# Keeping the residual in the output rows and adding the last sums there by accumulating transfers

## The chip, the core and the metric

The kernel runs on one of the eight cores of a Trainium2 chip. A core has engines that run their own instruction lists side by side and wait for each other through semaphores: TensorE (PE in the profile, its weight loads PEld) multiplies matrices into PSUM, VectorE (DVE), ScalarE (ACT) and GpSimd (POOL) work element by element, and SyncE (SP) here only issues transfers. The metric is the device time of one launch in microseconds (us). Several runs were timed; one more execution was recorded by the profiler.

## The reference

One layer of a hybrid backbone on 128 context tokens and 512 latent tokens, 1,024 channels each. A mixer sub-layer (pooling and neighbourhood attention, merged by gates) gives a first residual, then a channel sub-layer adds to it. Cut to what matters here:

```python
x = x + ga * _merge(pool, na, gp, gn, w_pool_proj, w_na_proj, w_o)
h = _modulated_norm(x, norm_ffn_g, sf, cf)
x = x + gf * _conv_ffn(h, w_up, ffn_conv_w, ffn_conv_b, w_down)
```

`_conv_ffn` is an up-projection to 2 x 2,816 channels, a width-3 convolution over positions, `silu(a) * g`, and a down-projection. The change is about the last line: the `x` on its right is the residual, and its left side is the output, `y_prompt` for the context tokens (rows `yc`) and `y_sample` for the latent ones (rows `yl`).

## The kernel before

All matrices are float32. Each product is made of three matmuls on operands that are split into a high part and a remainder (`split_to`, L132: ACT casts the high part, L133, DVE subtracts it, L134). The 640 tokens are five tiles of 128: tile 0 the context, tiles 1 to 4 the latent tokens.

The end of the program is the channel sub-layer. `out_product` (L731) makes `x1`, the residual, tile by tile, and L742 stores each tile to a scratch tensor `xscr` in DRAM, since the buffers of `x1` are given up afterwards. The up-projection then runs in 22 blocks of 128 + 128 channels (`up_a`, `up_w`, `products_b`, `up_b`). Each block multiplies in a scheme with fewer products: POOL forms four combinations `ws` of its weights (L858 to L861, `up_a`), `up_w` splits them, `products_b` multiplies and combines the results into `ua` and `ug` (`ug` at L887 by DVE, with a copy `p5` of a partial product by ACT, L885). `up_b` then convolves (`conv`: ACT at L925, DVE taps at L926 and L927), applies silu (ACT, L942), multiplies (L943, POOL, for the last block DVE) and splits into `ahi` and `alo` (in the last block `th` and `tl`, in the place of older tiles).

Two blocks make a group for the down-projection: `down_weights` loads and splits its two weight tiles, `down_group` multiplies and adds into an SBUF tile `acc` of five token tiles by 1,024. There are 11 groups. Up to group 8 (`GATED`) the sums are added without the gate `gf`. Then `join` (L952) runs over all ten pieces of `acc` (five tiles, two halves of 512 columns): POOL multiplies the piece with the gate (L953), SP loads the piece of the residual back from `xscr` into one of three small buffers `xr` (L955), and POOL adds it (L956). Group 9, and tile 0 of group 10, multiply the new sum with the gate on DVE (L998) and add it on POOL (L999). The other tiles of group 10 use weights that were multiplied with the gate beforehand (POOL, L973), so DVE only adds (L1001). SP stores each finished piece to the output (L1006); tile 4 goes in pieces of 256 columns.

Weights come through `load_raw` (L124) into three buffers `raw` of 512 KB; the gated weight tiles take buffers of the same three. A load waits until the buffer's last reader is done, and all plain transfers stand in one list on SP, in order. The order of each engine's instructions is set ahead of the run by a scheduler that works from a model of the machine, so a change in one place can reorder the instructions around it on several engines. The program was recorded with `schedule_with_timeline_sim=True`.

Of the kernel before, what the change touches and what calls it, by code (L numbers as in the profile page):

```python
# [10 lines left out]
F32 = mybir.dt.float32  # L11
# [6 lines left out]
P = 128  # L18
D = 1024
# [40 lines left out]
def tok_cols(t):  # L60
    return slice(t * P, (t + 1) * P)
# [3 lines left out]
def body(ctx, tc, A):  # L65
    nc = tc.nc
    MULT, ADD, SUB, MIN = ALU.mult, ALU.add, ALU.subtract, ALU.min
# [6 lines left out]
    def pool(stack, name, bufs=1, side="left", space=bass.MemoryType.SB):  # L74
        return stack.enter_context(tc.tile_pool(name=name, bufs=bufs, space=space, reuse_waits="tile",
                                                side=side if space == bass.MemoryType.SB else None))
# [16 lines left out]
    mraw = const.tile([P, 4, 2, 8], F32, name="mraw")  # L93
    dscr = pool(ctx, "dscr", space=bass.MemoryType.DRAM)
    gscr = dscr.tile([2, 16, P], F32, name="gscr")
    xscr = dscr.tile([P, 5, D], F32, name="xscr")
    qg8 = const.tile([P, 1], F32, name="qg8")
    nc.vector.tensor_scalar(out=bca1[:, 0:8], in0=vec[:, V_BCA:V_BCA + 8], scalar1=1.0, scalar2=None, op0=ADD)
    nc.vector.tensor_scalar(out=qg8, in0=vec[:, V_QG:V_QG + 1], scalar1=DH ** -0.5, scalar2=None, op0=MULT)
# [13 lines left out]
    def ps_acc():  # L113
        return PS.tile([P, 512], F32, tag="acc", name="acc", bufs=NACC)
# [224 lines left out]
    for t in range(5):  # L339
        dst = VX if t == 0 else V[t - 1]  # L340
# [293 lines left out]
    for g in range(4):  # L634
        d = pool_group(g)
# [55 lines left out]
    x1 = fp.tile([P, 5, D], F32, name="x1")  # L691
# [17 lines left out]
    def residual(ps, t, chunk, sq):  # L709
        sl = slice(chunk * 512, (chunk + 1) * 512)  # L710
        tmp = fp.tile([P, 512], F32, name="o_t", bufs=2)
        nc.vector.tensor_tensor(out=tmp, in0=ps, in1=gab[:, 1 if t == 0 else 0, sl], op=MULT)
        if chunk == 0:
            nc.gpsimd.tensor_tensor(out=x1[:, t, sl], in0=x1[:, t, sl], in1=tmp, op=ADD)
        else:
            nc.vector.tensor_tensor(out=x1[:, t, sl], in0=x1[:, t, sl], in1=tmp, op=ADD)
        nc.scalar.activation(tmp, x1[:, t, sl], AF.Square, accum_out=sq[:, t:t + 1])
# [6 lines left out]
    for u in range(4):  # L724
        r = load_raw(A["wo"][4 + u])
        sl = slice(2 * u, 2 * u + 2)
        split_to(two(r), w1h[:, sl, :], w1l[:, sl, :])
    for t in range(5):
        residual(acc[t], t, 0, sq0)

    def out_product(t, mid):  # L731
        ps = ps_acc()
        for kt in range(KT):
            if kt == MID and t:
                mid(t - 1)
            xh, xl = mhi[:, kt, tok_cols(t)], mlo[:, kt, tok_cols(t)]
            nc.tensor.matmul(ps, lhsT=xh, rhs=w1h[:, kt, :], start=(kt == 0), stop=False)
            nc.tensor.matmul(ps, lhsT=xh, rhs=w1l[:, kt, :], start=False, stop=False)
            nc.tensor.matmul(ps, lhsT=xl, rhs=w1h[:, kt, :], start=False, stop=(kt == KT - 1))
        residual(ps, t, 1, sq1)  # L740

        nc.sync.dma_start(xscr[:, t, :], x1[:, t, :])  # L742
        std = fp.tile([P, 1], F32, name="std2", bufs=2)
        nc.vector.tensor_tensor(out=std, in0=sq0[:, t:t + 1], in1=sq1[:, t:t + 1], op=ADD)
        nc.scalar.activation(std, std, AF.Sqrt, bias=eps, scale=1.0 / D)
        nc.vector.reciprocal(std, std)
        xn = fp.tile([P, D], F32, name="xn2", bufs=2)
        nc.scalar.activation(xn, x1[:, t, :], AF.Copy, scale=std)
        return xn
# [56 lines left out]
    for t in range(5):  # L806
        xns.append(out_product(t, lambda t: second_h(t, xns[t])))
        if t >= 3:
            sums(*J[t - 3])
# [141 lines left out]

    def join(o, gate, t, sl):  # L952
        nc.gpsimd.tensor_tensor(out=o, in0=o, in1=gate, op=MULT)  # L953
        xr = fr.tile([P, 512], F32, tag="xr", name="xr", bufs=3)
        nc.sync.dma_start(xr, xscr[:, t, sl])  # L955
        nc.gpsimd.tensor_tensor(out=o, in0=o, in1=xr, op=ADD)  # L956

    def down_weights(g):
# [20 lines left out]
    def down_group(g, xs, ws, gated):  # L979
        last = g == NG - 1  # L980
        for t in range(5):
            c0 = 0 if t == 0 else C_LAT - 1 + (t - 1) * P
            n = CUT if last and t == 4 else 512
            for c in range(0, D, n):
                sl = slice(c, c + n)
                ps = (ps_acc if g >= NG - 2 and (c // 512 + t) % 2 else ps_small)()[:, :n]
                for j, (hi, lo) in enumerate(gated if last and t else ws):
                    xh, xl = [x[:, c0:c0 + P] for x in xs[j]]
                    nc.tensor.matmul(ps, lhsT=xh, rhs=hi[:, sl], start=(j == 0), stop=False)  # L989
                    nc.tensor.matmul(ps, lhsT=xh, rhs=lo[:, sl], start=False, stop=False)  # L990
                    nc.tensor.matmul(ps, lhsT=xl, rhs=hi[:, sl], start=False, stop=(j == GRP - 1))  # L991
                o = acc[:, t, sl]
                gate = gfb[:, 1 if t == 0 else 0, sl]
                if g == 0:
                    nc.vector.tensor_copy(o, ps)
                elif g > GATED and (t == 0 or not last):
                    tmp = fr.tile([P, 512], F32, tag="xr", name="xr", bufs=3)
                    nc.vector.tensor_tensor(out=tmp, in0=ps, in1=gate, op=MULT)  # L998
                    nc.gpsimd.tensor_tensor(out=o, in0=o, in1=tmp, op=ADD)  # L999
                else:  # L1000
                    nc.vector.tensor_tensor(out=o, in0=ps, in1=o, op=ADD)  # L1001
                if g == GATED:
                    gating.append((o, gate, t, sl))
                if last:
                    dst = A["yc"] if t == 0 else A["yl"][(t - 1) * P:t * P, :]
                    nc.sync.dma_start(dst[:, sl], o)  # L1006

    pend = []
    for f in range(NF):
        if 1 < f + 1 < NF:  # L1010
            up_a(f + 1)
        nxt = up_b(f)
        if 1 < f + 1 < NF:
            up_w(f + 1)
        if f == NF - 2:
            for a in gating[5:]:
                join(*a)
        elif f == NF - 3:
            for a in gating[:5]:
                join(*a)  # L1020
        g = f // GRP - 1
        if f >= NF - 2:
            pend.append(nxt)
            continue
        if f % GRP == 0 and g >= 0:
            down_group(g, pend, *down_weights(g))
            pend = []
        pend.append(nxt)
    w2, w1 = down_weights(NG - 2), down_weights(NG - 1)
    with tc.issue_after(upped[0]):  # L1030
        down_group(NG - 2, pend[:GRP], *w2)
    down_group(NG - 1, pend[GRP:], *w1)
    e6.close()

# [96 lines left out]
```

## Time and profile before

| | us |
|---|---|
| median of 3 runs | 928.6 (926.58 to 931.41) |
| the profiled execution | 925.25 |
| its span, first to last instruction | 923.5 |
| PE busy in the span | 873.9 (95%) |
| DVE busy | 680.4 (74%) |
| ACT busy | 397.0 (43%) |
| POOL busy | 280.3 (30%) |

The span is what the trace covers; the profiled execution's own time is 1.75 us longer. A matmul counts as busy until its modelled end, so a busy PE says that PE wasn't waiting, not that it ran at its peak. The shares are averages over very different stretches; over the last tenth of the span they say little. In the rows, L and a number is a line of the kernel, `x10` a count, and `[4.28 <-ACT whi L133]` says that the engine had been idle for 4.28 us and which instruction's end released it.

### The profile page before, as it was taken

Reading aid. Unit: us, or ns where it says so; the run is one execution under the profiler, and the core shown is the slowest. Engines: PE = TensorE matmul, PEld = TensorE weight load, DVE = VectorE, ACT = ScalarE, POOL = GpSimd, SP = SyncE. Lnnn points to the kernel's source line nnn. Section 1 sums busy time; section 2 is a strip of 40 time slices with the busy share of each in tenths; the row PEclk is TensorE's granted clock in tenths of the full one; section 3 lists DMA queues with packets and bytes.
Section 4 is the critical chain, followed back from the end, with each engine's and each line's share of the span. In section 5 each row is a group of like instructions: output and inputs, shape, how many; then the busy total and the mean of one; then the engine's idle time right before and its main releaser. Section 6 shows DMA issues by size and latency. Waiting matters only on the chain.

```text
span 923.5 us, 13399 instructions
## 1 busy us (share of the span) xinstructions
PE 873.9 (95%) x5234; PEld 783.5 (85%) x5234; DVE 680.4 (74%) x998; ACT 397.0 (43%) x712; POOL 280.3 (30%) x206
## 2 busy tenths in 40 slices
PE   3799999999998999999889899999999999999688
PEld 2578898887898999988689799999999999898677
DVE  3456986897479633535699888879788797887696
ACT  4351344445443422225766453635435354453340
POOL 2122000000000021322206434444334543339956
PEclk9999999999999999999989999999999999999989
DMA  8758425664365222264222421213222141222213
GB/s 235 248 206 270 153 75 171 200 227 137 104 197 159 73 84 73 70 233 155 92 69 103 137 78 59 92 61 122 70 69 92 46 136 51 89 92 80 92 45 115
DMA packets 33024, 112.20 MB, mean 121 GB/s; under 512 B 3857, under 2 KB 4529, under 8 KB 32705
## 3 DMA queue, kind: packets, MB, share of 16 engines
q1 hardware_dynamic: 31840, 107.91, 35.5%
q0 software_dynamic: 1120, 3.44, 1.3%
q8 instruction: 41, 0.67, 0.3%
q14 instruction: 23, 0.18, 0.1%
HBM read 104.50 MB, written 5.78 MB: 119 GB/s over the span
## 4 chain that ended last, share of the span: by engine, by line
PE 75%; DMA 8%; DVE 8%; POOL 4%; issue 3%; ACT 2%; SPq 0%; DVEq 0%; ACTq 0%; POOLq 0%
PE acc L836 22%; PE acc L219 20%; PE sm L989 4%; PE sm L990 4%; PE sm L991 4%; PE acc L203 3%; PE acc L205 3%; PE acc L204 3%; DVE wlo L134 2%; DMA na<-in_xl 2%; POOL acc L953 2%; DMA raw<-in_wo 2%; DVE cv L926 1%; DMA raw<-in_wup 1%; PE sm L541 1%
## 5 line engine op out<-in xcount | busy, mean ns | idle before, releaser
L133 ACT CAST whi<-raw 128x1024 fp32r<-128x1024 f32 (+1 forms) x86 | 81.2, 946 | 192.3 <-PE acc L836 73.6
L134 DVE TENSOR_TENSOR wlo<-raw,whi 128x1024 fp32r<-128x1024 f32 (+1 forms) x86 | 104.4, 1215 | 39.7 <-ACT whi L133 38.8
L836 PE MATMUL acc<-th,whi 128*128 128x322 f32 (+1 forms) x336 | 104.8, 316 | 7.0 <-ACT whi L133 4.3
L836 PE MATMUL acc<-th,wlo 128*128 128x322 f32 (+1 forms) x336 | 105.6, 315 | 1.3 <-DVE wlo L134 1.3
L836 PE MATMUL acc<-tl,whi 128*128 128x322 f32 (+1 forms) x336 | 105.4, 314 | 0.0
L219 PE MATMUL acc<-hhi,whi 128*128 128x320 f32 x320 | 91.7, 320 | 0.4 <-ACT t L440 0.4
L219 PE MATMUL acc<-hlo,whi 128*128 128x320 f32 x320 | 89.5, 313 | 0.0
L219 PE MATMUL acc<-hhi,wlo 128*128 128x320 f32 x320 | 88.6, 313 | 0.0
L858 POOL TENSOR_TENSOR ws<-raw 128x512 f32<-128x512 f32 x21 | 30.2, 1438 | 168.8 <-DVE wlo L134 104.3
L989 PE MATMUL sm<-dhi,ahi 128*128 128x512 f32 x190 | 72.6, 397 | 3.6 <-ACT dhi L133 1.7
L990 PE MATMUL sm<-dlo,ahi 128*128 128x512 f32 x190 | 75.1, 395 | 0.0
L836 PEld LDWEIGHTS acc<-th,whi 128*128 128x128 f32 x336 | 63.9, 191 | 10.3 <-ACT whi L133 5.8
L991 PE MATMUL sm<-dhi,alo 128*128 128x512 f32 x190 | 72.4, 395 | 0.0
L836 PEld LDWEIGHTS acc<-th,wlo 128*128 128x128 f32 x336 | 64.4, 192 | 3.1 <-DVE wlo L134 1.8
L836 PEld LDWEIGHTS acc<-tl,whi 128*128 128x128 f32 x336 | 64.3, 191 | 1.5
L133 ACT CAST whi<-ws 128x1024 fp32r<-128x1024 f32 x42 | 43.2, 1046 | 51.3 <-PE acc L836 41.0
L134 DVE TENSOR_TENSOR wlo<-ws,whi 128x1024 fp32r<-128x1024 f32 x42 | 53.6, 1292 | 13.3 <-ACT whi L133 13.3
L1001 DVE TENSOR_TENSOR acc<-sm,acc 128x512 f32<-128x512 f32 (+1 forms) x85 | 55.8, 676 | 9.2 <-PE sm L991 9.0
L836 PE MATMUL acc<-b1l,whi 128*128 128x322 f32 x184 | 57.8, 316 | 3.8 <-DVE b1l L134 3.8
L219 PEld LDWEIGHTS acc<-hhi,whi 128*128 128x128 f32 x320 | 58.2, 191 | 2.8 <-issue 1.3
L219 PEld LDWEIGHTS acc<-hlo,whi 128*128 128x128 f32 x320 | 58.2, 191 | 0.8 <-issue 0.7
L836 PE MATMUL acc<-b1h,whi 128*128 128x322 f32 x184 | 57.5, 316 | 0.8 <-ACT b1h L133 0.8
(322 smaller groups left out, 2313.6 us busy)
## 6 DMA issues: line engine op xcount, KB each, us to landing
raw<-in_wup SPq DMA_DIRECT2D x44, 512.0 KB, 4.6
mw<-in_wmT SPq DMA_DIRECT2D x32, 512.0 KB, 4.6
raw<-in_wdn SPq DMA_DIRECT2D x22, 512.0 KB, 3.4
raw<-in_wmt SPq DMA_DIRECT2D x20, 512.0 KB, 3.5
raw<-in_wm SPq DMA_DIRECT2D x16, 512.0 KB, 9.3
raw<-in_wtok SPq DMA_DIRECT2D x12, 512.0 KB, 11.6
bias<-in_bias SPq DMA_DIRECT2D x16, 384.0 KB, 4.7
raw<-in_wab SPq DMA_DIRECT2D x8, 512.0 KB
```

What stands on the lines that cost most here:

```text
L133: nc.scalar.copy(hi, raw)
L134: nc.vector.tensor_tensor(out=lo, in0=raw, in1=hi.bitcast(F32), op=SUB)
L203: nc.tensor.matmul(ps[t], lhsT=xh, rhs=wh, start=(kt == 0), stop=False)
L204: nc.tensor.matmul(ps[t], lhsT=xh, rhs=wl, start=False, stop=False)
L205: nc.tensor.matmul(ps[t], lhsT=xl, rhs=wh, start=False, stop=(kt == KT - 1))
L219: nc.tensor.matmul(o[:, :n], lhsT=w[:, k], rhs=cut(x, k, c, n), start=st and a, stop=sp and b)
L836: upped[0] = nc.tensor.matmul(ps[:, cs], lhsT=a[:, c], rhs=b[:, k, cs], start=start and first, stop=last, skip_group_check=skip and not st ...
L858: nc.gpsimd.tensor_tensor(out=s[:, 1], in0=a21, in1=a22, op=ADD)
L989: nc.tensor.matmul(ps, lhsT=xh, rhs=hi[:, sl], start=(j == 0), stop=False)
L990: nc.tensor.matmul(ps, lhsT=xh, rhs=lo[:, sl], start=False, stop=False)
L991: nc.tensor.matmul(ps, lhsT=xl, rhs=hi[:, sl], start=False, stop=(j == GRP - 1))
L1001: nc.vector.tensor_tensor(out=o, in0=ps, in1=o, op=ADD)
```

## The change

The scratch `xscr` shrinks to one tile. The residual of tiles 0 to 3 is stored to the output rows, at the place in SP's list where it went to the scratch; tile 4 still goes to the scratch. `join` keeps the product with the gate for all ten pieces, but reloads and adds the residual only for the two of tile 4. At the end, the eight pieces of tiles 0 to 3 are no longer stored by SP but added to the output rows by transfers with `accum_op=ADD`, which POOL issues; each names the store of its tile's residual as something to wait for.

```diff
-    xscr = dscr.tile([P, 5, D], F32, name="xscr")
+    xscr = dscr.tile([P, D], F32, name="xscr")
...
+    waiting = []
+
+    def y_rows(t):
+        return A["yc"] if t == 0 else A["yl"][(t - 1) * P:t * P, :]
...
-        nc.sync.dma_start(xscr[:, t, :], x1[:, t, :])
+        if t < 4:
+            waiting.append(nc.sync.dma_start(y_rows(t), x1[:, t, :]).ins)
+        else:
+            nc.sync.dma_start(xscr, x1[:, t, :])
...
     def join(o, gate, t, sl):
         nc.gpsimd.tensor_tensor(out=o, in0=o, in1=gate, op=MULT)
+        if t < 4:
+            return
         xr = fr.tile([P, 512], F32, tag="xr", name="xr", bufs=3)
-        nc.sync.dma_start(xr, xscr[:, t, sl])
+        nc.sync.dma_start(xr, xscr[:, sl])
         nc.gpsimd.tensor_tensor(out=o, in0=o, in1=xr, op=ADD)
...
                 if last:
-                    dst = A["yc"] if t == 0 else A["yl"][(t - 1) * P:t * P, :]
-                    nc.sync.dma_start(dst[:, sl], o)
+                    if t < 4:
+                        d = nc.gpsimd.dma_start(y_rows(t)[:, sl], o, accum_op=ADD).ins
+                        tc.add_manual_dep(d, waiting[t].name,
+                                          mybir.DependencyInfo(mybir.DependencyClass.Sync, mybir.DependencyReason.DATA),
+                                          reason="the residual is there before the sum is added to it")
+                    else:
+                        nc.sync.dma_start(y_rows(t)[:, sl], o)
```

The scheduler's order is the same on all engines up to the joins. From there it moves; three places follow. The lines of the changed kernel are 8 to 10 higher (L953 is L961 there, L956 L966, L861 L869, L887 L895).

POOL before, from the last block's first combination to the last gated weight tile (`ws` are the combinations, L953 and L956 the joins):

```order
L858 TENSOR_TENSOR ws<-raw 128x512
L860 TENSOR_TENSOR ws<-raw 128x512
L956 TENSOR_TENSOR acc<-acc,xr 128x512
L953 TENSOR_TENSOR acc<-acc,gfb 128x512
L956 TENSOR_TENSOR acc<-acc,xr 128x512 x2
L859 TENSOR_TENSOR ws<-ws,raw 128x512
L943 TENSOR_TENSOR cv<-cv 128x642
L956 TENSOR_TENSOR acc<-acc,xr 128x512
L861 TENSOR_TENSOR ws<-raw,ws 128x512
L973 TENSOR_TENSOR raw<-raw,gfb 128x1024
L943 TENSOR_TENSOR cv<-cv 128x642
L973 TENSOR_TENSOR raw<-raw,gfb 128x1024
```

The same engine and place now, from the first join to the end of POOL's work:

```order
L961 TENSOR_TENSOR acc<-acc,gfb 128x512 x3
L951 TENSOR_TENSOR cv<-cv 128x642
L961 TENSOR_TENSOR acc<-acc,gfb 128x512 x6
L966 TENSOR_TENSOR acc<-acc,xr 128x512
L866 TENSOR_TENSOR ws<-raw 128x512
L868 TENSOR_TENSOR ws<-raw 128x512
L961 TENSOR_TENSOR acc<-acc,gfb 128x512
L867 TENSOR_TENSOR ws<-ws,raw 128x512
L966 TENSOR_TENSOR acc<-acc,xr 128x512
L869 TENSOR_TENSOR ws<-raw,ws 128x512
L951 TENSOR_TENSOR cv<-cv 128x642
L983 TENSOR_TENSOR raw<-raw,gfb 128x1024 x2
```

Two additions are left of ten, one ahead of the combinations and one among them. Before, nine of the additions stood ahead of L859.

DVE before, ahead of the `ug` addition of the last block (`ug0_4536` from `acc_8216`), for which PE's last up products wait:

```order
L134 TENSOR_TENSOR dlo_8453<-raw_8450,dhi_8452 128x1024
L134 TENSOR_TENSOR wlo3_8341<-raw_8210,whi3_8340 128x512
L134 TENSOR_TENSOR wlo_8337<-ws_8245,whi_8336 128x1024
L926 SCALAR_TENSOR_TENSOR cv_8322<-ug0_4536,vec_66,cv_8322 128x642
L927 SCALAR_TENSOR_TENSOR cv_8322<-ug0_4536,vec_66,cv_8322 128x642
L134 TENSOR_TENSOR b1l_4036<-raw_8456,b1h_4035 128x1024
L887 TENSOR_TENSOR ug0_4536<-acc_8216,p5_8391 128x320
L134 TENSOR_TENSOR wlo_8463<-raw_8460,whi_8462 128x1024
L889 TENSOR_TENSOR ua1_4535<-acc_8364,u2_8377 128x320
```

DVE now, ahead of the same addition (`ug0_4536` from `acc_8201`):

```order
L134 TENSOR_TENSOR wlo_8439<-raw_8436,whi_8438 128x1024
L934 SCALAR_TENSOR_TENSOR cv_8307<-ug0_4536,vec_66,cv_8307 128x642
L897 TENSOR_TENSOR ua1_4535<-acc_8340,u2_8353 128x320
L134 TENSOR_TENSOR b1l_4036<-raw_8442,b1h_4035 128x1024
L935 SCALAR_TENSOR_TENSOR cv_8307<-ug0_4536,vec_66,cv_8307 128x642
L134 TENSOR_TENSOR wlo_8449<-raw_8446,whi_8448 128x1024
L934 SCALAR_TENSOR_TENSOR cv_8408<-ua1_4535,vec_66,cv_8408 128x642
L895 TENSOR_TENSOR ug0_4536<-acc_8201,p5_8367 128x320
L935 SCALAR_TENSOR_TENSOR cv_8408<-ua1_4535,vec_66,cv_8408 128x642
```

The addition has moved behind both splits of the last group's weights (`b1l` twice, `wlo` of the gated tiles `raw_8436` and `raw_8446`) and behind one tap of the last block.

POOL now, at the end of its list; before, the twelve L999 were the last:

```order
L1009 TENSOR_TENSOR acc<-acc,xr 128x512 x12
L1016 DMA out_yc<-acc 128x512
L1016 DMA out_yl<-acc 128x512
L1016 DMA out_yc<-acc 128x512
L1016 DMA out_yl<-acc 128x512 x5
L1142 UNCONDITIONAL_BRANCH
```

Eight transfers were added there. SP keeps the four stores of tile 4 and stores nothing else at the end.

## Rows read from the trace of the kernel before

**Rows 1.** Busy time by stretch: start:end, length, each engine's busy time, granted clock, DMA
```profile
700.00:860.00 160.00, 158.63 (x931) 147.07 (x931) 133.01 (x146) 73.64 (x106) 80.20 (x50) 1.00 0.27 88
...
863.00:892.00 29.00, 17.00 (x88) 15.29 (x87) 22.02 (x20) 13.40 (x18) 23.49 (x13) 0.89 0.24 81
```

**Rows 2.** Timeline of PE, 848 to 889 us: start, length, instruction, idle before
```profile
848.45 0.50 PE L989 MATMUL sm<-dhi,ahi 128*128 128x512 f32 x1 [1.37 <-DVE acc L1001]
...
862.85 0.31 PE L836 MATMUL acc<-tl,whi 128*128 128x322 f32 x1
863.00 0.31 PE L836 MATMUL acc<-th,wlo 128*128 128x322 f32 x1
...
866.37 0.41 PE L836 MATMUL acc<-b2h,whi 128*128 128x320 f32 x1 [3.06 <-ACT p L885]
...
874.44 0.41 PE L836 MATMUL acc<-th,whi 128*128 128x322 f32 x1 [4.28 <-ACT whi L133]
...
888.67 0.42 PE L836 MATMUL acc<-th,whi 128*128 128x322 f32 x1 [2.17 <-DVE ug L887]
```

**Rows 3.** POOL, 835 to 892 us, by line (first three), then its timeline
```profile
L956 POOL TENSOR_TENSOR acc<-acc,xr 128x512 f32<-128x512 f32 x10 | 17.9, 1799 | 0.0
L953 POOL TENSOR_TENSOR acc<-acc,gfb 128x512 f32<-128x512 f32 x10 | 16.0, 1610 | 0.0
L973 POOL TENSOR_TENSOR raw<-raw,gfb 128x1024 f32<-128x1024 f32 x2 | 6.2, 3102 | 3.8 <-DMA raw<-in_wdn 3.8
...
834.20 1.71 POOL L861 TENSOR_TENSOR ws<-raw,ws 128x512 f32<-128x512 f32 x1
...
877.00 1.87 POOL L861 TENSOR_TENSOR ws<-raw,ws 128x512 f32<-128x512 f32 x1
```

**Rows 4.** Timeline of ACT
```profile
864.94 1.04 ACT L133 CAST dhi<-raw 128x1024 fp32r<-128x1024 f32 x1 [4.20 <-DMA raw<-in_wdn]
...
873.34 1.04 ACT L133 CAST whi<-ws 128x1024 fp32r<-128x1024 f32 x1 [7.03 <-POOL ws L859]
```

**Rows 5.** Timeline of DVE
```profile
874.42 1.48 DVE L134 TENSOR_TENSOR wlo<-ws,whi 128x1024 fp32r<-128x1024 f32 x1 [5.50 <-ACT whi L133]
...
879.48 0.88 DVE L927 SCALAR_TENSOR_TENSOR cv<-ua,vec,cv 128x642 f32<-128x642 f32 x1
...
881.41 0.68 DVE L134 TENSOR_TENSOR wlo<-raw,whi 128x512 fp32r<-128x512 f32 x1
882.01 1.21 DVE L134 TENSOR_TENSOR wlo<-ws,whi 128x1024 fp32r<-128x1024 f32 x1
883.14 3.02 DVE L926 SCALAR_TENSOR_TENSOR cv<-ug,vec,cv 128x642 f32<-128x642 f32 x1
...
888.14 0.48 DVE L887 TENSOR_TENSOR ug<-acc,p 128x320 f32<-128x320 f32 x1
...
893.95 0.82 DVE L134 TENSOR_TENSOR alo<-cv,ahi 128x642 fp32r<-128x642 f32 x1
```

**Rows 6.** SP's issues around 861 us
```profile
861.38 0.33 SPq L126 DMA_DIRECT2D raw<-in_wdn  x1
```

**Rows 7.** The end: timelines of POOL and DVE, and SP's stores with median us to landing
```profile
899.81 16.27 POOL L999 TENSOR_TENSOR acc<-acc,xr 128x512 f32<-128x512 f32 x11 [1.37 <-DVE xr L998]
...
920.19 0.42 DVE L1001 TENSOR_TENSOR acc<-acc 128x256 f32<-128x256 f32 x1 [0.21 <-PE acc L991]
...
out_yl<-acc SPq DMA_DIRECT2D x6, 256.0 KB, 2.4
```

**Rows 8.** Transfers that POOL issues: its time for one, and us to landing
```profile
72.22 0.93 POOL L345 DMA_DIRECT2D out_new_v<-vv  x1 [11.67 <-ACT vv L344]
...
73.70 0.54 POOL L408 DMA_DIRECT2D ck<-in_ckT  x1
...
out_new_v<-vv POOLq DMA_DIRECT2D x1, 256.0 KB, 7.9
```

**Rows 9.** The chain of waits at 888 us
```profile
888.67 3.28 PE acc L836 x12
```

## Prediction

> **What bounds the kernel now.** I read the busy time by stretch first. From 700 to 860 us TensorE (PE) works 158.63 of 160 us at granted clock 1.00; from 863 to 892 it works 17.00 of 29 us, and the clock there is 0.89, so part of that stretch ran at 1.2 GHz instead of 2.4 [rows 1]. Up to 860 us the kernel is thus bound by PE's own work, and nothing that the change does to other engines there can shorten it. The 12.0 us of idle PE behind it can go. PE's own rows say who ended the idle times: ACT's copy of a partial product (3.06 us), ACT's cast of the combined weights (4.28), and, at the end, a VectorE (DVE) add into `ug` (2.17); the rest are short, and one of 1.37 stands earlier, at 848 us [rows 2].
>
> Then POOL. It ends the combinations `ws` of the last-but-one block at 834.20 + 1.71 = 835.9 us and those of the last block only at 877.00 + 1.87 = 878.9; between them it works without a gap, and the ten products with the gate (16.0 us) and the ten additions of the residual (17.9 us) are 34 of those 43 us [rows 3]. ACT shows the consequence: its cast of `ws` stood 7.03 us behind POOL, and PE behind the cast; its earlier wait, 4.20 us, was for a load of down weights, not for POOL [rows 4]. Last DVE: from 874.42 it runs its work in one piece until the `ug` add ends at 888.14 + 0.48 = 888.6, and that add releases PE's last twelve up products and, behind them, the down products [rows 2, 5]. So two things stand in a row: POOL holds the weights until 874, and DVE then needs 14.2 us to catch up.
>
> **The change part by part.**
>
> *Residual written to the output rows.* Four stores go to `yc`/`yl` instead of the scratch, at the same place in SP's order, with the same size. Cost 0; the fifth is unchanged. Nothing before 835.9 us differs in any engine's order, so the sum starts there.
>
> *Eight additions and eight reloads leave POOL and SP.* From 835.9 to 878.9 POOL ran 26 operations (10 products, 10 additions, 2 conv products L943, 4 combinations), 43.0 us, 1.65 us each. Now 17 stand there (10, 2, 1 and 4): 17 x 1.65 = 28.1 us, so `ws` is whole at about 864.0 instead of 878.9. That is 14.9 us of POOL, but PE can't take them all; what is late next is the rest of this walk.
>
> *ACT.* Ahead of the two casts of `ws` stands, now as before, the cast of the first down weights, whose load goes out at 861.38, when DVE releases the buffer, and which begins at 864.94 [rows 4, 6]. With the 1.37 us of PE at 848 regained it begins at 863.6 and ends at 864.6. The two casts end at 866.7, the copy behind them (0.42) at 867.1. PE, which stops at 863.31 now, would be there at 861.9 and has 12 products left, 0.15 us from start to start [rows 2], 1.8 us; it waits from 863.7 to 866.7: 3.0 us, as much as its first wait now. The second one (4.28) is gone.
>
> *DVE.* From 864.6 on its new order holds, up to and with that same `ug` add, 8 splits of 1,024 columns, 5 conv taps, `alo`, one split of 512 and 4 adds from PSUM: 8 x 1.21 + 5 x 0.88 + 0.82 + 0.68 + 4 x 0.48 = 17.5 us when nothing disturbs them [rows 5]. POOL disturbs them: a tap that takes 0.88 took 3.02 beside the product with the down weights [rows 5]. From 874.42 to 888.6 the same kinds of work, 4 x 1.21 + 4 x 0.88 + 0.82 + 0.68 + 0.48 = 10.3 us, took 14.2: 3.9 lost, beside one addition, one combination, one L973 and most of an L943. In the new stretch POOL has two L973 (3.1 each [rows 3]) and two L943, about as much, so I take 3.9 again. The `ug` add ends at 864.6 + 17.5 + 3.9 = 886.0, against 888.6: gain 2.6 us. PE waits there for it from about 877.5, longer than its 2.17 now. So DVE, off the path while POOL was late, becomes the bound, and most of POOL's 14.9 us turn into a longer last wait.
>
> *Bounds of that term.* Were nothing lost to POOL, the add would end at 882.1: gain 6.5. Were each of POOL's four operations beside it to cost what the worst pair shows, 3.02 - 0.88 = 2.1 us, 8.6 would be lost instead of 3.9, and the add, with the 1.4 us of the first load not regained either, would end at 892.1: 3.5 slower. I take 2.6: the stretch that it is read from has the same engines, lines and shapes.
>
> *The tail.* Behind PE's restart nothing in the amount of PE's work changes: 28 us of down products, then a DVE add that ends at 920.19 + 0.42 and a store of 128 to 256 KB that lands 2.4 us after its issue [rows 7]. All of it moves by 2.6. New there is POOL: behind its twelve L999, which end at 899.81 + 16.27 = 916.1 and now at 913.5, it issues eight accumulating transfers of 256 KB. No row shows one. Nearest are POOL's plain issues: 0.54 us for a load by rows, 0.93 for a store in short pieces [rows 8]; landing 2.4 us, as SP's store, and 7.9 (`new_v`, at 72 us) [rows 7, 8]. The eighth is issued at 913.5 + 7 x 0.54 = 917.3 and lands at 919.7; the last plain store of token tile 4 lands at 920.6 + 2.4 - 2.6 = 920.4. So the cover is SP's own last store, with 0.7 us to spare, and the tail costs 0. The rule: with issue d and landing L it stays hidden while 7d + L < 6.9, and eats the gain of 2.6 at 9.5. At 0.93 and 7.9 it is 14.4: 7.5 us over, 4.9 slower in all. That each waits for the residual's store to the same rows costs nothing: those stores stand ahead of the first up products.
>
> The Trainium skill, "DMA: Bandwidth & Descriptors", section "Latency and other measured facts", gives the POOL path about 1 us to the first byte for software emission, against 0.6 on SP's. Taken as d, that estimate would make 7 + 2.4 = 9.4, the gain gone. POOL's plain rows, at 0.54 to 0.93, stand below it.
>
> **Sum.** 925.25 (span 923.5 and 1.75 around it) - 2.6 = 922.65 for the profiled execution. The median of the three runs is 928.6, 3.35 above it; the same difference gives 926.0.
>
> **The rivals.**
>
> *B: DVE is not held up.* With eight additions gone POOL leaves DVE alone, the add ends at 882.1 and PE's shorter idle keeps the clock up. The twelve products behind the add took 3.28 us [rows 9] and at 0.15 each need 1.8: up to 1.5 more. Gain 6.5 + 1.5 = 8.0: 920.6. For it: taps at 3.02 and 0.88 in one stretch [rows 5]. Against it: the two L973 remain, and they are the long ones. A gain of all 12.0 + 1.4 us would need a DVE that never binds; its 17.5 us of work forbid it.
>
> The Trainium skill, "SBUF — State Buffer", section "Who interferes with whom", says that a DVE instruction with two SBUF inputs and a GpSimd instruction that reads SBUF exclude each other, the later one fully blocked. The 3.02 us agree. By it alone every removed POOL operation gives DVE its time back, up to 10 us, and it is B that would come.
>
> *C: the accumulating transfers end the kernel.* POOL issues each as slowly as the store in short pieces and they land as late as `new_v`: 4.9 us slower, 933.5. It decides from 7d + L = 9.5 on. For it: reading and adding at the destination is more work than any row shows, and they are POOL's last eight instructions. Against it: they are whole rows of 512 values, not short pieces.
>
> *D: the joins were not what held POOL.* If its time goes into waits for the group's sums instead, `ws` comes little earlier, and the gain is 0: 928.6. Against it: POOL had no gap in 43 us [rows 3].
>
> **How the numbers follow.** My forecast 0.55 (own range 922 to 930), B 0.27, C 0.12, D 0.06. The most that a measurement of this kernel can tell from no change is about 0.5%, 4.6 us. Faster than that: B but for 0.02, and 0.07 of mine: 0.32. Slower: most of C and a little beside it: 0.10. Within: 0.58. Range: B's 920.6 less what single runs of before lie below their median, 2.0 us, gives 918 or so; above, the slow bound of my own term lies at 932.1 and C at 933.5, of which half is left out: 931.5.
>
> **What would show it.** Right: POOL's last L861 ends near 864 instead of 878.9; PE's wait on the cast of `ws` at 874 gone; one PE wait of 7 to 9 us ended by the DVE `ug` add, near 886; DVE without a gap before it; POOL's eight issues near 0.54 us, done before PE's last product; SP's last store landing last. Wrong: PE's longest wait behind 860 us not on `ug`, but on a load of down weights or on POOL; or the span ending more than 4 us behind PE's last product, on an accumulating transfer.

## The result and the profile after

The changed kernel takes 933.75 us (median of 12 runs, 928.89 to 941.33), the kernel before, in runs taken with it, 929.07: ratio 1.0058 (95% interval 1.0032 to 1.0084), so about 5.4 us slower. The forecast was 926.0 with a range of 918 to 931.5; the result lies outside it, at rival C's 933.5. The profiled execution of the changed kernel took 932.59 us with a span of 930.8.

The two executions differ by 7.3 us, and not all of that is the change. Up to POOL's first product of a sum with the gate (L953, now L961) every engine has the same order in both kernels, and yet it stands at 835.87 us in one and at 838.23 in the other: executions scatter by that much ahead of the change. I therefore count from this product. The columns are the start of the product, then, from there, the end of the last `ug` addition on DVE, the end of the last addition at the end of the kernel, and the end of the span; each is a row's start plus its length, minus the first column.

| kernel | product with the gate | last `ug` | last sum | end | end behind last sum |
|---|---|---|---|---|---|
| before | 835.87 | 52.75 | 84.74 | 87.63 | 2.89 |
| changed | 838.23 | 51.85 | 83.87 | 92.57 | 8.70 |

From there the change costs 92.57 - 87.63 = 4.94 us: 0.90 are gained up to the `ug` addition, nothing moves between it and the last sum, and 5.81 are lost behind the last sum. These are one trace each; the traces below show that such distances scatter by 0.7 us at the `ug` addition and by 1.5 at the last sum, so the loss stands clear of the scatter and the gain barely does.

**Ahead of 890 us the forecast mechanism is there.** The stretches of the changed kernel that answer to [rows 1], and PE's waits from 800 us on (engine, what was waited for: us in total, times, longest):

```profile
700.00:860.00 160.00, 159.06 (x934) 147.37 (x933) 132.27 (x147) 74.58 (x107) 78.96 (x49) 1.00 0.24 80
863.00:892.00 29.00, 16.71 (x94) 16.00 (x94) 28.00 (x24) 15.49 (x20) 14.63 (x7) 0.85 0.22 73
```

```profile
PE acc L844 <- DVE ug L895: 8.0, 1, 8.0
PE acc L844 <- ACT whi L133: 4.3, 1, 4.3
```

POOL's work from 863 to 892 fell from 23.49 to 14.63 us, but PE's did not rise (17.00, 16.71): DVE's went from 22.02 to 28.00 of 29. PE's granted clock is 0.85 there, was 0.89. PE has one long wait of 8.0 us, on the `ug` addition, as forecast. Of the waits in [rows 2], those of 3.06 and 4.28 have become one, on the casts of `ws` (PE's timeline):

```profile
869.47 0.43 PE L844 MATMUL acc<-th,whi 128*128 128x322 f32 x1 [4.25 <-ACT whi L133]
```

POOL's timeline, with the last combination and the two products with the down weights, and DVE's up to the addition:

```profile
865.55 1.85 POOL L869 TENSOR_TENSOR ws<-raw,ws 128x512 f32<-128x512 f32 x1
...
874.51 2.40 POOL L983 TENSOR_TENSOR raw<-raw,gfb 128x1024 f32<-128x1024 f32 x1 [4.62 <-DVE dlo L134]
881.63 2.96 POOL L983 TENSOR_TENSOR raw<-raw,gfb 128x1024 f32<-128x1024 f32 x1 [4.72 <-DMA raw<-in_wdn]
```

```profile
867.13 1.35 DVE L134 TENSOR_TENSOR dlo<-raw,dhi 128x1024 fp32r<-128x1024 f32 x1 [0.46 <-ACT dhi L133]
868.51 3.60 DVE L134 TENSOR_TENSOR wlo<-ws,whi 128x1024 fp32r<-128x1024 f32 x2
...
874.70 3.29 DVE L134 TENSOR_TENSOR b1l<-raw,b1h 128x1024 fp32r<-128x1024 f32 x1
...
882.70 2.96 DVE L134 TENSOR_TENSOR b1l<-raw,b1h 128x1024 fp32r<-128x1024 f32 x1
...
889.60 0.48 DVE L895 TENSOR_TENSOR ug<-acc,p 128x320 f32<-128x320 f32 x1
```

The last L869 ends at 867.4 where the last L861 ended at 878.9 [rows 3]. From 867.13 DVE has no gap and ends the addition at 890.1. Both `b1l` splits, 1.21 us of work each, take about 3 beside POOL's two products.

**The loss is at the end.** POOL's eight issues answer to [rows 8], here the first three and the eighth one by one, with the landing of the first and of the eighth (the last figure, us):

```profile
913.63 0.86 POOL L1016 DMA_DIRECT2D out_yc<-acc  x1
914.23 1.17 POOL L1016 DMA_DIRECT2D out_yl<-acc  x1
914.81 1.48 POOL L1016 DMA_DIRECT2D out_yc<-acc  x1
915.35 5.36 POOL L1016 DMA_DIRECT2D out_yl<-acc  x5
...
919.84 0.86 POOL L1016 DMA_DIRECT2D out_yl<-acc  x1
...
out_yc<-acc POOLq DMA_DIRECT2D x1, 256.0 KB, 3.6
...
out_yl<-acc POOLq DMA_DIRECT2D x1, 256.0 KB, 9.0
```

The first ones follow each other by 0.54 to 0.60 us, as forecast. The last three wait for their pieces: DVE's sums end at 916.74, 918.14 and 919.54 and the issues start 0.30 us behind each, the eighth at 919.84. What grows is the time to landing, from 3.6 us for the first transfer to 9.0 for the eighth. The DMA part of the page for 913 to 930.8 us (queue: packets, MB, share of 16 engines; then issues, KB each, median us to landing), and the stretches of the end (the last two figures of a row are DMA's share and GB/s; a packet counts whole in the stretch in which it starts, so a share can pass 1):

```profile
q0 software_dynamic: 1152, 2.10, 72.5%
q1 hardware_dynamic: 576, 0.52, 9.6%
out_yl<-acc POOLq DMA_DIRECT2D x6, 256.0 KB, 8.2
out_yc<-acc POOLq DMA_DIRECT2D x2, 256.0 KB, 5.1
```

```profile
915.00:919.00 4.00, 4.00 (x20) 3.28 (x19) 1.88 (x4) 0.00 (x0) 4.00 (x6) 1.00 1.06 148
919.00:923.00 4.00, 2.65 (x23) 2.44 (x21) 2.24 (x5) 0.00 (x0) 1.66 (x2) 1.00 1.09 180
923.00:927.00 4.00, 0.00 (x0) 0.00 (x0) 0.00 (x0) 0.00 (x0) 0.00 (x0) 0.67 1.13 221
927.00:930.80 3.80, 0.00 (x0) 0.00 (x0) 0.00 (x0) 0.00 (x0) 0.00 (x0) 0.50 0.39 112
```

The accumulating transfers occupy all 16 DMA engines for 0.725 x 17.8 = 12.9 us, 1.6 us each, at 2.10 MB / 12.9 us = 163 GB/s. The engines are full from 915 to beyond 927 while PE has been done since 921.7. SP's four stores of tile 4 are caught in the same line: in the trace the last accumulating packet ends at 928.4 us and the last packet of SP's stores at 929.1, and the span 1.7 behind that. Before, the stores at the end had this row, 2.62 MB in 0.672 x 10.5 = 7.1 us, 371 GB/s (DMA part for 913 to 923.5 us):

```profile
q1 hardware_dynamic: 1728, 2.62, 67.2%
```

### The profile page after: what moved, and what is told of

It reads as the page before. It is cut to its first block, busy times and chain, and to the rows that moved or that the text cites. A ratio compares the mean times of both kernels' runs of the same rounds, so it can differ in the third digit from the quotient of the medians.

```text
span 930.8 us, 13369 instructions
## 1 busy us (share of the span) xinstructions
PE 872.1 (94%) x5234; PEld 783.2 (84%) x5234; DVE 676.0 (73%) x998; ACT 397.0 (43%) x712; POOL 275.4 (30%) x206
## 4 chain that ended last, share of the span: by engine, by line
PE 70%; DVE 10%; DMA 9%; POOL 4%; ACT 4%; issue 2%; SPq 0%; DVEq 0%; ACTq 0%; POOLq 0%
PE acc L219 19%; PE acc L844 19%; PE sm L999 4%; PE sm L1000 4%; PE sm L1001 4%; PE acc L203 3%; PE acc L205 3%; PE acc L204 3%; DVE wlo L134 3%; DMA na<-in_xl 2%; ACT whi L133 2%; POOL acc L961 2%; DMA raw<-in_wdn 2%; DMA raw<-in_wo 2%; DVE cv L934 2%
## 5 line engine op out<-in xcount | busy, mean ns | idle before, releaser
L866 POOL TENSOR_TENSOR ws<-raw 128x512 f32<-128x512 f32 x21 | 33.2, 1583 | 168.2 <-DVE wlo L134 96.0
L999 PE MATMUL sm<-dhi,ahi 128*128 128x512 f32 x190 | 72.4, 397 | 3.1 <-ACT dhi L133 1.7
L219 PEld LDWEIGHTS acc<-hhi,wlo 128*128 128x128 f32 x320 | 57.6, 190 | 0.7 <-issue 0.5
## 6 DMA issues: line engine op xcount, KB each, us to landing
raw<-in_wtok SPq DMA_DIRECT2D x12, 512.0 KB, 11.5
```

The source lines that it names most:

```text
L219: nc.tensor.matmul(o[:, :n], lhsT=w[:, k], rhs=cut(x, k, c, n), start=st and a, stop=sp and b)
L866: nc.gpsimd.tensor_tensor(out=s[:, 1], in0=a21, in1=a22, op=ADD)
```

## The experiments

Theory T: the loss is the eight accumulating transfers, because they fill the DMA engines at the end of the kernel. Theory D: what POOL gave back went into PE's wait on DVE's walk to the `ug` addition. The medians of one kernel carry about 0.25% of uncertainty; where less decides, I read the distances of the table, one trace each. Two traces of one kernel (e4) differ by 0.02 us at the `ug` addition and by 0.79 at the last sum; the four kernels whose order up to there is the changed one (changed, e1, e2, e5) have 51.75 to 52.49 at the `ug` addition, so 0.3 to 1.0 us less than before, and 83.87 to 85.33 at the last sum.

| kernel | median us | ratio to before (95%) | `ug` | last sum | end behind it |
|---|---|---|---|---|---|
| e1 plain stores by SP | 927.61 | 0.9997 (0.9970 to 1.0023) | 51.75 | 84.08 | 2.60 |
| e2 plain stores by POOL | 926.93 | 0.9992 (0.9967 to 1.0017) | 51.89 | 84.20 | 2.59 |
| e5 whole rows | 936.01 | 1.0074 (1.0046 to 1.0102) | 52.49 | 85.33 | 6.89 |
| e4 two tiles | 934.69 | 1.0061 (1.0034 to 1.0087) | 53.20 | 85.00 | 5.04 |
| e4, second trace | 931.51, one run | | 53.18 | 85.79 | 4.29 |
| e3 sums in SBUF | 930.05 | 1.0019 (0.9996 to 1.0041) | 54.63 | 87.57 | 2.78 |
| e7 = e1, late splits | 924.43 | 0.9946 (0.9922 to 0.9970) | 46.93 | 79.63 | 3.68 |
| e8 = before, late splits | 929.39 | 1.0011 (0.9984 to 1.0039) | 51.83 | 83.77 | 4.77 |
| e9 additions behind `ws` | 928.14 | 0.9991 (0.9968 to 1.0015) | 51.93 | 84.99 | 2.66 |
| e6 = e1, no gate product | 925.04 | 0.9951 (0.9918 to 0.9984) | 47.75 | 81.00 | 2.65 |
| g1 additions on DVE | 928.40 | 1.0010 (0.9982 to 1.0038) | 47.04 | 84.30 | 5.33 |
| f4 sums in SBUF, 5 transfers | 923.70 | 0.9952 (0.9927 to 0.9978) | 46.93 | 81.18 | 2.74 |

**e1 and e2: the same kernel, plain stores at the end.**

```
-  d = nc.gpsimd.dma_start(y_rows(t)[:, sl], o, accum_op=ADD).ins
+  d = nc.sync.dma_start(y_rows(t)[:, sl], o).ins       # e1
+  d = nc.gpsimd.dma_start(y_rows(t)[:, sl], o).ins     # e2
```

> The changed kernel, but the last group's eight pieces of the four tiles go out as plain stores from SP, so the residual is left out of those rows; the order on PE, DVE and ACT is that of the changed kernel. Theory T (the eight accumulating transfers at the end are the loss: 2.10 MB took 12.9 us of all 16 DMA engines, from 915 to 928.5): the span ends as before's does, some 2.9 us behind the last DVE add, 924.5 instead of 930.8; about 927.5 us, ratio to before 0.998 to 1.000. Theory L (the loss stands ahead of 890 us, PE restarts at 890.1 instead of 888.7, and the tail is hidden): no change against the changed kernel, 933 to 934, ratio 1.005. The forecast as made (DVE's walk shorter by 2.6 us): 926, ratio 0.997.

> The changed kernel, but the eight transfers on POOL at the end are plain stores (no addition at the destination; the residual is left out of those rows). Every engine's order is that of the changed kernel. T, by the addition: plain packets of 2 KB take about 65 ns as the stores at the end of the kernel before do, not 179, the eight take under 6 us of the DMA engines, and the end is set by the eighth issue, 919.8 plus about 3: 928 to 930 us, ratio 0.999 to 1.001. Rival Q (POOL's software queue is slow with any transfer): as slow as the changed kernel, 933 to 934.

Both leave out the residual of tiles 0 to 3, which the stores overwrite, and both come back to the time of before: with the same work ahead of it the end shrinks from 8.70 to 2.6 us, whoever issues. T holds, and L (a loss ahead of 890 us) falls; Q, the slow queue of POOL, falls too. e2's DMA part for 910 to 932 us, and three of its issues:

```profile
q0 software_dynamic: 640, 2.10, 25.2%
...
out_yl<-acc POOLq DMA_DIRECT2D x6, 256.0 KB, 2.7
```

```profile
917.61 0.55 POOL L1016 DMA_DIRECT2D out_yl<-acc  x1
918.15 0.54 POOL L1016 DMA_DIRECT2D out_yc<-acc  x1
...
923.54 0.54 POOL L1016 DMA_DIRECT2D out_yl<-acc  x1 [0.86 <-DVE acc L1011]
```

The same bytes from the same queue take 0.252 x 22 = 5.5 us of the engines instead of 12.9, an issue takes 0.54 us and lands 2.7 later; here too the last issues wait for DVE's sums. It is the addition at the destination that makes the transfers 2.3 times as long. They went in fewer packets than the accumulating ones (640, not 1152), but that isn't it: e5 has 576 with the addition.

**e5: half as many transfers, the same bytes.** For `t < 4`, one transfer once both halves of a tile are summed:

```
-  d = nc.gpsimd.dma_start(y_rows(t)[:, sl], o, accum_op=ADD).ins
+  d = nc.gpsimd.dma_start(y_rows(t), acc[:, t, :], accum_op=ADD).ins    # only with the second half
```

> The changed kernel with one accumulating transfer of 128 x 1024 per token tile at the end instead of two of 128 x 512: four instead of eight, the same bytes. If the DMA engines' time goes by bytes: 12.9 us again, started no earlier than now, 933 to 935. If it goes by packet: half the packets, 6.5 us, the end near 925: 928 to 929 us. If POOL's issues were what spaces them (0.6 to 0.9 us each): four issues fewer, 2.5 to 3 us less than the changed kernel: 930 to 931.

936.0 (7 runs): the price goes nearly by bytes. In its DMA part for 910 to 932 us

```profile
q0 software_dynamic: 576, 2.10, 52.4%
```

half the packets take 0.524 x 22 = 11.5 us, 182 GB/s, 2.1 times e2's 5.5. Half the packets and half the issues save a tenth of it, so neither sets the time. The last transfer starts later, since it needs the whole row; counted from the product with the gate the end is at 92.22 us, in the changed kernel at 92.57.

**e4: half as many bytes.** `t < 2` in place of `t < 4`; tiles 2 to 4 are joined as before (10 runs).

> The changed kernel with the residual written to the output rows for token tiles 0 and 1 only: four accumulating transfers at the end, tiles 2 to 4 joined on POOL as before. T (8 transfers take 12.9 us of the DMA engines, 1.6 each): four take 6.5, from about 915 to 922, hidden behind the last sums and plain stores: 927 to 929, ratio 0.998 to 1.001. Rival (any accumulating transfer at the end has a long fixed latency, 8 us from issue to landing): the last of the four, issued near 916, lands at 924 and the end stays 1 to 2 us late: 929.5 to 931, ratio 1.002 to 1.003.

> A second trace of the kernel with four accumulating transfers at the end. Its first one showed, behind POOL's first product with the gate, the ug addition at 53.2 us (before 52.75, changed kernel 51.85), the last sum at 85.0, and the end 5.0 us behind the last sum (before 2.9, changed 8.7): 2.4 us more than before in all. If that is its cost, the second trace shows 53, 85 and 4.5 to 5.5 again, and what its median of 934.7 has beyond that came from ahead of 835 us. If four transfers cost as much as eight: 7 us or more behind the last sum.

The dose is seen in the transfers (in the second trace, 905 to 935 us, 0.218 x 30 = 6.5 us for four), but my 927 to 929 was wrong: the end stays 4.3 to 5.0 us behind the last sum, because the plain stores share the engines with what is left of them. The rival, a fixed latency of some 8 us, is out by the changed kernel's first transfer, which landed after 3.6. The second trace's DMA part:

```profile
q0 software_dynamic: 576, 1.05, 21.8%
q1 hardware_dynamic: 1152, 1.57, 14.8%
...
out_yl<-acc SPq DMA_DIRECT2D x4, 256.0 KB, 4.9
```

SP's stores land after 4.9 us instead of 2.4 [rows 7]. The Trainium skill, "DMA: Bandwidth & Descriptors", section "Issuing engines are not separate DMA queues", says that transfers of SP, ACT and POOL run on the same 16 engines and interleave; the two queues here agree. From the table e4 should cost 90.04 - 87.63 = 2.4 us; its median shows 5 to 6 more than before. What it has beyond 2.4 lies ahead of the product with the gate or is scatter, and stays open.

**e3: the additions as transfers into SBUF, early.** In the kernel before, the reload and POOL's addition become one accumulating transfer:

```
-  nc.sync.dma_start(xr, xscr[:, t, sl])
-  nc.gpsimd.tensor_tensor(out=o, in0=o, in1=xr, op=ADD)
+  nc.gpsimd.dma_start(o, xscr[:, t, sl], accum_op=ADD)
```

> The kernel before, with the ten additions of the residual on POOL (and the reloads into a buffer) replaced by ten accumulating transfers from the scratch into the sums in SBUF, issued by POOL at the same places, 840 to 880 us; the last group's pieces go out by plain stores as before. If T holds (what hurts is only that the additions stand at the end): POOL is relieved (ten issues of 0.6 to 0.9 us for ten additions of 1.79), the tail is before's, and the gain of the earlier weights, 0.9 us seen in the changed kernel, stays: 927 to 929, ratio 0.997 to 1.000. If an accumulating transfer costs wherever it stands (its 16 us of DMA engines delay the weight loads, or POOL's issues hold up DVE): 930 to 934, ratio over 1.002.

The end is short again (2.78), but the walk is 1.9 us longer than before's; 930.05 us is at the lower edge of the second case, the ratio between the two. POOL, by line, from 820 us on, and one split on DVE:

```profile
L954 POOL DMA_DIRECT2D acc<-xscr x10 | 12.6, 1482 | 0.0
```

```profile
859.49 4.43 DVE L134 TENSOR_TENSOR wlo<-raw,whi 128x1024 fp32r<-128x1024 f32 x1 [0.44 <-ACT whi L133]
```

POOL is relieved: an issue lasts 1.48 us, but the next operation begins about 0.6 us behind its start, and the last L861 ends 35.7 us behind the product with the gate (43.0 before, 29.2 in the changed kernel). DVE is not: this split of 1.21 us takes 4.43, the first load of the down weights goes out 31.1 us behind that product instead of 25.5, and the walk is late with it. Whether POOL's issues beside the split held it, or the operations between them, this run doesn't show.

**e7 and e8: the walk of DVE.** The splits of the last down group are queued behind the last `ug` addition, in e1's kernel (e7) and in the kernel before (e8):

```
-  w2, w1 = down_weights(NG - 2), down_weights(NG - 1)
+  w2 = down_weights(NG - 2)
+  with tc.issue_after(ugged[0]):       # the last ug addition of products_b
+      w1 = down_weights(NG - 1)
```

> The plain-store kernel (the changed kernel, its last eight pieces stored plainly by SP, so the residual is left out of those rows), with the weights of the last down group split only behind the last ug addition on DVE. Two splits b1l (3.29 and 2.96 us in the changed kernel's trace) and two of the weights with the gate (1.2 each) leave DVE's walk to that addition. Theory D (what POOL gave back turned into PE's one wait of 8.0 us on that addition, because DVE's walk ends it): the walk is 4.8 us shorter undisturbed, 8.7 as measured, the wait falls from 8.0 to 0 to 3 us, and the kernel takes 920 to 923, ratio 0.991 to 0.995. Rival W (PE would wait there all the same, on POOL's combinations, on a load, or later on the weights moved back): no change against the plain-store kernel, 927 to 929.

> The kernel before with the same move alone: the last down group's splits behind the last ug addition on DVE, the ten residual additions left on POOL. D: POOL still ends the combinations at 878.9, and only one b1l of 1.22 us stood ahead of the ug addition behind them, so 0 to 1.5 us: 926.5 to 928.5, ratio 0.998 to 1.000. Rival (the order on DVE alone is the gain, POOL's relief isn't needed): as much as in the plain-store kernel, 5 to 6 us, ratio 0.994.

e7 is 0.9946 of before, at the slow edge of the 0.991 to 0.995 expected, and its 924.43 us above the 920 to 923; PE's waits from 800 us on:

```profile
PE acc L844 <- ACT whi L133: 4.3, 1, 4.3
PE acc L844 <- DVE ug L895: 2.1, 1, 2.1
```

8.0 has become 2.1, the walk 46.93 us. D holds. In the kernel before the same move gives 0.9 us of walk, and nothing that its time shows. Of the walk, POOL's relief alone is worth 0.3 to 1.0, the move alone 0.9, both together 5.8: behind POOL stood DVE, and each hides the other.

Not all of it reaches the end. In e8 the last sum comes before SP is through its list of stores:

```profile
915.22 4.48 SPq L1006 DMA_DIRECT2D out_yl<-acc  x8
```

Its last issue starts at 919.30 us, 1.9 behind the last sum; in the kernel before the two stood 0.03 apart. So the span of e8 ends 88.5 us behind the product with the gate, before's 87.6, and that of e7 83.3: 4.3 of the 5.8 arrive.

**e6: does POOL hold DVE?** e1 with `r2 = r` instead of POOL's product of the down weights with the gate, which is left out.

> The plain-store kernel without POOL's two products of the down weights with the gate (left out: the last group of tiles 1 to 4 is not gated). In the trace of the changed kernel DVE's two b1l splits beside these took 3.29 and 2.96 us instead of 1.21. If POOL's operations hold DVE up (3.9 us of loss in the forecast, 5.4 measured): the walk from POOL's first product with the gate to the ug addition falls from 51.8 to 47 to 49 us, PE's wait of 8.0 falls by as much, 923 to 925.5, ratio 0.994 to 0.997. Rival (the walk is long by its own work; the long operations are a matter of records): 51 or more, 927 to 929.

The walk falls by 4.0 us, 51.75 to 47.75. In e1 a split and a tap stood beside the two products (in the changed kernel it was two splits):

```profile
875.09 3.29 DVE L134 TENSOR_TENSOR b1l<-raw,b1h 128x1024 fp32r<-128x1024 f32 x1
...
882.45 2.58 DVE L934 SCALAR_TENSOR_TENSOR cv<-ug,vec,cv 128x642 f32<-128x642 f32 x1 [0.61 <-ACT cv L933]
```

In e6 both splits take 1.21 and 1.22, and that tap 0.88:

```profile
879.85 1.21 DVE L134 TENSOR_TENSOR b1l<-raw,b1h 128x1024 fp32r<-128x1024 f32 x1
...
886.00 1.22 DVE L134 TENSOR_TENSOR b1l<-raw,b1h 128x1024 fp32r<-128x1024 f32 x1
```

The Trainium skill, "SBUF — State Buffer", section "Who interferes with whom", says that a DVE instruction with two SBUF inputs and a GpSimd instruction that reads SBUF exclude each other. These rows agree: 2.96 to 3.29 us beside a product of 2.4 to 3.0, 1.21 without.

**e9 and g1: the additions elsewhere.** e9 is e8 with the ten additions on POOL queued behind the last `ws`; g1 is e8 with the eight of tiles 0 to 3 on DVE in the last down group, from reloads of whole rows:

```
+  with tc.issue_after(combined[0]):    # e9: the last combination ws
+      for a in gating: join_add(*a)
+  nc.vector.tensor_tensor(out=o, in0=o, in1=res[:, sl], op=ADD)    # g1: ahead of the last group's sum
```

> The kernel before, with the last down group's splits behind the last ug addition on DVE, and the ten residual additions on POOL put behind the last combination ws instead of ahead of it: nothing of the work is left out, no accumulating transfer. D: ws is whole near 868 as in the changed kernel, the additions (18 us) fill POOL's gaps of 870 to 890; they disturb DVE there, by 3 to 5 us of the 5 to 8 that the move is worth, and POOL ends its twelve additions of the last groups no later than 916: 922 to 927, ratio 0.994 to 0.999. Rival (the additions beside DVE's walk cost as much as they give): 928 to 930, ratio 1.000 or more.

> The whole computation, no accumulating transfer. The residual of tiles 0 to 3 goes to the scratch as before; its eight additions leave POOL's stretch of 836 to 879 us, and stand on DVE behind 897 us (0.68 us each, 5.4 in all, in a stretch in which DVE works 16.5 of 29 us), from four reloads of 512 KB; the last down group's splits stand behind the last ug addition. If the two findings add up (POOL's relief counts once DVE's walk is cleared, and the end must not carry the additions by transfers): ug addition 47 us behind POOL's first product with the gate, as in the plain-store kernel with that move, the end 2.6 to 3.7 us behind the last sum: 922 to 925, ratio 0.992 to 0.997. Rival (eight more DVE operations beside POOL's twelve additions delay the last sums by as much): 927 to 930, ratio 0.999 or more.

Neither gains: 922 to 927 and 922 to 925 us were forecast, 928.14 and 928.40 came, as the rivals had it. In e9 POOL's additions stand beside the walk and DVE pays (51.93, not 46.93):

```profile
871.08 2.56 DVE L134 TENSOR_TENSOR wlo<-ws,whi 128x1024 fp32r<-128x1024 f32 x1
873.56 2.30 DVE L134 TENSOR_TENSOR dlo<-raw,dhi 128x1024 fp32r<-128x1024 f32 x1
```

In g1 the walk is short (47.04), and the last sums are late by as much: beside POOL's twelve additions DVE's took up to 1.77 us each, not 0.68, and POOL waited for DVE in turn:

```profile
916.88 1.77 DVE L998 TENSOR_TENSOR acc<-acc,raw 128x512 f32<-128x512 f32 x1
```

```profile
914.62 3.48 POOL L1004 TENSOR_TENSOR acc<-acc,xr 128x512 f32<-128x512 f32 x2 [1.23 <-DVE xr L1003]
```

**f4: the version that beats both.** The whole computation: plain stores at the end, the late splits of e7, and the residual added in SBUF by five accumulating transfers behind the last `ws`.

```
+  with tc.issue_after(combined[0]):
+      for t in range(5):
+          nc.gpsimd.dma_start(acc[:, t, :], xscr[:, t, :], accum_op=ADD)
```

> The whole computation. The ten residual additions on POOL are replaced by five accumulating transfers of 128 x 1024 from the scratch into the sums in SBUF, issued by POOL right behind the last combination ws (near 868 us); the last down group's splits stand behind the last ug addition. The five move 2.6 MB, some 16 us of the 16 DMA engines, from 870 to 887, and must land before POOL's additions of 898. If an accumulating transfer costs its engine time alone: the walk is that of the plain-store kernel with the same move (46.9 us), 923 to 926, ratio 0.994 to 0.998. Rival (its issue or its writes into SBUF hold up DVE, as a split of 1.21 us took 4.43 beside such issues in the run with ten of them): 3 to 5 us are lost again, 927 to 930.

0.9952 of before, 0.9927 to 0.9978. The five issues take POOL 4.47 us. In the DMA part for 860 to 936 us the transfers occupy the engines for 0.176 x 76 = 13.4 us and land after 14.6 in the median, the last near 884, where nothing waits for them; POOL's first addition of the last groups stands at 896.4:

```profile
863.32 4.47 POOL L1017 DMA_DIRECT2D acc<-xscr  x5
```

```profile
870.38 2.35 DVE L134 TENSOR_TENSOR wlo<-ws,whi 128x1024 fp32r<-128x1024 f32 x2
```

```profile
q0 software_dynamic: 720, 2.62, 17.6%
...
acc<-xscr POOLq DMA_DIRECT2D x5, 512.0 KB, 14.6
raw<-in_wdn SPq DMA_DIRECT2D x4, 512.0 KB, 8.8
```

Two splits take 2.35 us while they are under way, and the walk is e7's 46.93 us, so neither the issues nor the writes into SBUF held DVE here; the rival falls. The transfers slow the loads of the down weights to 8.8 us, from 3.5 in the page of the changed kernel, and PE waits 5.3 instead of 4.3 us on the casts:

```profile
PE acc L836 <- ACT whi L133: 5.3, 1, 5.3
PE acc L836 <- DVE ug L887: 2.5, 1, 2.5
```

The last sum comes at 81.18 us, 1.6 later than in e7, where the residual is left out, and the end at 83.9, 0.6 later.

## Why the prediction was wrong

**The step that failed is the tail**: "So the cover is SP's own last store, with 0.7 us to spare, and the tail costs 0." It measured 5.81 us. The eighth issue stood where the forecast had it: 917.3 - 835.87 = 81.4 us behind the product with the gate, measured 81.6. That was luck: POOL's additions ended 75.4 us behind the product, not 77.6, and the last issues then waited for DVE's sums, which the forecast left out. The price of a plain transfer was right too (e2: issue 0.54, landing 2.7 against 2.4). Wrong was the landing L, taken as 2.4 us for each of the eight. They share the 16 DMA engines, which were a third resource that the sum left out; with the addition each occupies them for 1.6 us, so the last landing is the start plus eight times that: 915 + 12.9 = 927.9, and with SP's four stores between them (0.096 x 17.8 = 1.7 us) 929.6; the trace's last packet ends at 929.1. The first transfer landed after 3.6 us, the eighth after 9.0, from standing in line. The cover itself went the same way: SP's last store shares the engines and does land last, but 90.8 us behind the product with the gate where the forecast had 84.5. What the prediction named as the sign of this came true in the main: the span ends 9 us behind PE's last product, with accumulating transfers filling the engines until 0.7 us before the last packet. The bound used for L, `new_v` at 7.9 us [rows 8], was of a transfer in short pieces alone.

**Rival C had the sign and the size, but only part of the cause.** 4.9 us slower, 933.5, by issues as slow as the store in short pieces and landings as late as `new_v`. The reason that I gave for it, "reading and adding at the destination is more work", is what e1 and e2 show. Its sum of 14.4 us is near the 6.2 + 9.0 = 15.2 from the first issue to the last landing, but that is luck: the last issues are paced by DVE's sums, as in e2, and a landing of 9.0 is a place in a line, not a latency. It had 0.12. What I held against it, whole rows instead of short pieces, doesn't touch the cost, which goes by bytes. The prediction's other estimate, 9.4 from 1 us for each issue, isn't what happened either: e2's issues took 0.54, and its end is 2.6 us behind the last sum.

**POOL: right.** Seventeen operations of 1.65 us were to take 28.1 us; from 838.23 to 867.40 they took 29.2.

**ACT: right in kind.** PE was to wait 3.0 us on the casts of `ws` and waited 4.25: counted from the first product with the gate, the casts came at 31.2 instead of 30.8 us, and PE stood there at 27.0 instead of 27.8. That there would be only this one wait ahead of the `ug` addition was right.

**DVE: right mechanism, size too small.** The walk was to begin 864.6 - 835.87 = 28.7 us behind the first product with the gate and began at 28.9; PE was to wait 7 to 9 us and waited 8.0. The term that was mis-sized is the loss to POOL: 890.08 - 867.13 = 22.95 us, less 17.5 of work, is 5.4 us, not 3.9; it made the gain 0.9 instead of 2.6 us. I had taken the loss of a stretch with one L973 for one with two. In e1's order e6 says that the two cost 4.0 us. So of the 7.5 us by which the change missed the forecast, a loss of 4.9 for a gain of 2.6, the tail is 5.8 and the walk 1.7.

**B fell for the reason named against it**: the two products remain. e7 shows what B forgot: the time was to be had on DVE, by what stands in its order ahead of the addition. **D** (the joins were not what held POOL) is out by POOL's own rows.

## What to carry to other kernels

A batch of transfers at the end of a kernel is priced by the time that it occupies the DMA engines, counted from its first issue, with every other store of the end in the same sum; latency and issue time give only the lower bound. An addition at the destination belongs where nothing waits for it soon: in f4 2.6 MB of it cost 1.6 us at the last sum and 0.6 at the end, in the tail 2.1 MB cost 5.8. And when the engine that binds is relieved, take the next one's order into the same change: POOL's relief was worth 0.3 to 1.0 us of walk until DVE's order was cleared, then 5.8 with it, 4.3 of them at the end.

## What the hardware showed beyond that

- An accumulating transfer moved 163 GB/s in rows of 2 KB and 182 in rows of 4 KB, a plain one from the same queue 2.10 MB / 5.5 us = 378.
- POOL's issue of an accumulating transfer of 128 x 512 lasted 0.86 us where it stood alone and up to 2.15 behind others (changed kernel), but the next issue or operation began 0.54 to 0.6 us behind its start (changed kernel, e3): its length in the trace isn't what it costs POOL.
- The same order of work reached POOL's first product with the gate between 833.66 us (e8) and 844.67 (g1). So executions scatter by up to 11 us ahead of the change. Distances from a common instruction scatter less: in the four kernels with the changed order by 0.7 us at the `ug` addition and 1.5 at the last sum.
